# Compression of keys and values: float16 halves under a power-of-two scale in place of 32-bit halves

## The chip, the cores and the metric

The kernel runs on one core of a Trainium2 chip. The metric is the device time of one execution in microseconds; the table below gives the median of three timed runs. A separate profiled execution of the same program gives the trace.

## What is computed

The reference is one inference step of a hybrid decoder layer for 2048 prompt tokens and 8 x 4 sample tokens: a norm, one wide input projection, a sparse attention (compressed, selected and window branches), a gated linear recurrence, gates, an output projection. The part that matters here is the compression of keys and of values into blocks:

```python
def compress(kv, pos, w1, w2):            # CMP_LEN 32, CMP_STRIDE 16, NSA_KV 2, NSA_HD 64, CMP_HID 64
    idx = np.arange(nc)[:, None] * CMP_STRIDE + np.arange(CMP_LEN)[None, :]
    blk = kv[:, idx] + pos[:, None, :]
    blk = jnp.swapaxes(blk, 2, 3).reshape(B, nc, NSA_KV, CMP_LEN * NSA_HD)
    out = jax.nn.silu(blk @ w1) @ w2
```

It runs on keys and on values, for the eight sample sequences (2048 past positions, gathered from pages) and for the prompt: nine sequences for each of the two kinds.

## The kernel before

The whole step is one program. Each product that needs more than half precision is written as three products of halves: high x high, low x high, high x low. The input projection keeps its operands as float16 halves under power-of-two scales (`load_w`, `pow2_scale`). Its matmuls are the program's filling: a generator (`projections`) hands out a few of them at a time, and other parts of the program call `fill(ns)` to put so many nanoseconds of them between their own steps. Lines 480 (token groups) and 399 (feature groups) are these matmuls. ScalarE and VectorE take their results out of two PSUM buffers.

The compression (`compression`, from line 1002) is driven by `along(compression(range(9)), 1900.0)`: after each of its steps 1900 ns of projection are put in. For each kind the weights `w1` are loaded as a 128 x 8 x 128 tile `raw` and cut into the halves `cwh` and `cwl` (lines 1017, 1018). Then, for each of nine sequences:

- the raw rows `xr` (128 x 2048) are gathered (line 996) or loaded (1040), two buffers in turn, and regrouped into `xg` by ScalarE (1045), for every fourth sequence by GpSimd (1043);
- four times, `turn` transposes four 128 x 128 pieces into the PSUM tile `pt` (1052), ScalarE copies it as the high half `Rh` (1056), and VectorE subtracts to get the low half `Rl` (1057); a turn is issued one step before its use;
- six matmuls for each turn (1069), 24 for a sequence, sum into `ph`; these are 432 in all;
- ScalarE and VectorE add the two shifted halves of `ph` into `hb` (1071, 1072), tanh and a small second product follow.

The helper `pow2_scale` transposes a column of row values on TensorE into a PSUM tile (`tp`, one buffer, shared with the projections), takes the maximum, clears the mantissa bits and inverts: one transpose and five small VectorE operations (lines 197 to 205).

The order of each engine's queue is decided by the scheduler of the language when the program is built. It goes by the program's order as priority and by a simulated timeline (`TC_ARGS = {"schedule_with_timeline_sim": True}`), so later work that is ready can move ahead of earlier work that isn't. On the chip the queues then run in that fixed order.

Of the kernel before, what the change touches and what calls it, by code (L numbers as in the profile page):

```python
# [10 lines left out]
F32 = mybir.dt.float32  # L11
F32R = mybir.dt.float32r
F16 = mybir.dt.float16
BF = mybir.dt.bfloat16
I32 = mybir.dt.int32
AF = mybir.ActivationFunctionType
OP = mybir.AluOpType
AX = mybir.AxisListType
# [122 lines left out]
def trunk_kernel(ctx: ExitStack, tc: tile.TileContext, A, O):  # L141
    nc = tc.nc
    pe, ve, ac, gp, sy = nc.tensor, nc.vector, nc.scalar, nc.gpsimd, nc.sync

    def f(ap):
        return ap.bitcast(F32)
# [48 lines left out]
    def pow2_scale(mx, pool, ps, tag):  # L195

        pe.transpose(ps[:, 0:128], mx.to_broadcast([128, 128]), ident)
        un = pool.tile([128, 1], F32, name=tag + "u", bufs=3)
        ve.tensor_reduce(un, ps[:, 0:128], axis=AX.X, op=OP.max)
        ve.tensor_scalar(un, un, TINY, None, op0=OP.max)  # L200
        ui = un.bitcast(I32)
        ve.tensor_scalar(ui, ui, 0x7F800000, None, op0=OP.bitwise_and)
        ve.tensor_scalar(un, un, 2.0 ** -14, None, op0=OP.mult)
        sc = pool.tile([128, 1], F32, name=tag + "s", bufs=3)
        ve.reciprocal(sc, un)
        return sc, un
# [7 lines left out]
    def track(col, src, rows=128):  # L214
        t_ = con.tile([128, 1], F32, name="trk", bufs=4)
        ve.tensor_reduce(t_[:rows], src, axis=AX.X if len(src.shape) == 2 else AX.XY, op=OP.max, apply_absolute_value=True)
        ve.tensor_tensor(mxs[:rows, col:col + 1], mxs[:rows, col:col + 1], t_[:rows], op=OP.max)
# [777 lines left out]
    def gather(dst, cache, b):  # L995
        gp.indirect_dma_start(out=dst, out_offset=None, in_=A[cache][0].rearrange("n (m l) g d -> (n m) (l g d)", l=16),
                              in_offset=bass.IndirectOffsetOnAxis(ap=idx[:, b:b + 1], axis=0))
# [6 lines left out]
    def compression(seqs):  # L1004
        with ExitStack() as st:
            cw = st.enter_context(tc.tile_pool(name="cw", bufs=1, side="right"))
            cp = st.enter_context(tc.tile_pool(name="cp", bufs=1, side="right"))
            cps = st.enter_context(tc.tile_pool(name="cps", bufs=1, space=PSUM, side="right"))
            ctp = st.enter_context(tc.tile_pool(name="ctp", bufs=3, space=PSUM, side="right"))
            for kind in "kv":  # L1010
                raw = cp.tile([128, 2048], F32, name="xr", bufs=2)[:, :1024].rearrange("p (j c) -> p j c", j=8)
                w1 = A["cmp_w1_" + kind][0]
                for a in range(2):
                    sy.dma_start(raw[:, :, a * 64:(a + 1) * 64], w1[a * 1024:(a + 1) * 1024].rearrange("(j p) c -> p j c", p=128))
                wh = cw.tile([128, 8, 128], F32R, name="cwh")
                wl = cw.tile([128, 8, 128], F32R, name="cwl")
                ac.activation(wh, raw, AF.Copy)
                ve.tensor_sub(wl, raw, f(wh))
                w2 = cw.tile([128, 128], F32, name="w2" + kind)
                ve.memset(w2, 0.0)  # L1020
                sy.dma_start(w2[:64, :64], A["cmp_w2_" + kind][0])
                ps = cw.tile([128, 16], F32, name="pos" + kind)
                sy.dma_start(ps, A["cmp_pos_" + kind][0].rearrange("(j a) d -> (a d) j", a=2))
                pc = cps.tile([64, 1], F32, name="p2")
                for l in range(16):
                    mm(pc, raw[:, l % 8, (l // 8) * 64:(l // 8 + 1) * 64], ps[:, l:l + 1], l == 0, l == 15)
                cb = cw.tile([64, 1], F32, name="cb" + kind)
                ve.tensor_copy(cb, pc)
                cn = cw.tile([64, 1], F32, name="cn" + kind)
                ve.tensor_scalar(cn, cb, 0.5, None, op0=OP.mult)  # L1030
                ve.tensor_scalar(w2[:64, :64], w2[:64, :64], 0.5, None, op0=OP.mult)
                hb_ = cw.tile([128, 2, 128], F32, name="hb" + kind)
                ve.memset(hb_, 0.0)
                hb = hb_[:64]
                for s in seqs:
                    xr = cp.tile([128, 2048], F32, name="xr", bufs=2)
                    if s < 8:
                        gather(xr, "cache_cmp_" + kind, s)
                    else:
                        sy.dma_start(xr, O["p_cmp_" + kind][0, 0].rearrange("(m l) g d -> m (l g d)", l=16))  # L1040
                    xg = cp.tile([128, 2, 16, 64], F32, name="xg", bufs=2)
                    if s % 4 == 3:
                        gp.tensor_copy(xg.rearrange("p g l d -> p l g d"), xr.rearrange("p (l g d) -> p l g d", g=2, d=64))
                    else:
                        ac.activation(xg.rearrange("p g l d -> p l g d"), xr.rearrange("p (l g d) -> p l g d", g=2, d=64), AF.Copy)
                    ph = cps.tile([128, 2, 128], F32, name="ph")

                    def turn(j2):
                        pt = ctp.tile([128, 4, 128], F32, name="pt")
                        for a in range(4):  # L1050
                            j, g = j2 * 2 + a // 2, a % 2
                            pe.transpose(pt[:, a], xg[:, g, 2 * j:2 * j + 2].rearrange("p a d -> p (a d)"), ident)  # L1052
                        Rh = cp.tile([128, 2, 2, 128], F32R, name="Rh", bufs=3)
                        Rl = cp.tile([128, 2, 2, 128], F32R, name="Rl", bufs=3)
                        ptv = pt.rearrange("p (j g) m -> p j g m", g=2)
                        ac.activation(Rh, ptv, AF.Copy)
                        ve.tensor_sub(Rl, ptv, f(Rh))
                        return Rh, Rl

                    nxt = turn(0)  # L1060
                    k = 0
                    for j2 in range(4):
                        Rh, Rl = nxt
                        if j2 < 3:
                            nxt = turn(j2 + 1)
                        yield
                        for j in range(2):
                            for l, r in ((wh, Rh), (wl, Rh), (wh, Rl)):
                                mm(ph, l[:, 2 * j2 + j], r[:, j], k == 0, k == 23)  # L1069
                                k += 1  # L1070
                    ac.activation(hb[:, :, :127], ph[64:128, :, 1:128], AF.Copy)
                    ve.tensor_add(hb[:, :, :127], hb[:, :, :127], ph[0:64, :, :127])
                    he = cp.tile([64, 2, 128], F32, name="he")[:, :, :127]
                    ac.activation(he, hb[:, :, :127], AF.Tanh, scale=0.5, bias=cn)
                    ve.tensor_scalar(he, he, 1.0, None, op0=OP.add)
                    ve.scalar_tensor_tensor(hb[:, :, :127], hb[:, :, :127], cb, he, op0=OP.add, op1=OP.mult)
                    yield
                    if kind == "k":
                        p2 = cps.tile([128, 2, 128], F32, name="p2")
                        mm(p2, w2, hb_, True, True)  # L1080
                        p2 = p2[:64]
                        if s < 8:
                            for g in range(2):
                                ve.tensor_copy(kcT[0][g * 64:(g + 1) * 64, s], p2[:, g])
                        else:
                            ve.tensor_copy(kcp, p2)
                            track(1, kcp[:, :, :127], 64)
                    else:
                        p2 = cps.tile([128, 2, 64], F32, name="p2")
                        for g in range(2):  # L1090
                            mm(p2[:, g], hb_[:, g], w2[:, :64], g == 0, True)
                        if s < 8:
                            ve.tensor_copy(vcs[0][:, s].rearrange("p (g d) -> p g d", g=2), p2)
                        else:
                            ve.tensor_copy(vcp, p2)
                            track(2, vcp[:127], 127)
# [1001 lines left out]
    with ExitStack() as s2:  # L2098
        sw, sb = ExitStack(), ExitStack()
        load_x, fill, state = make_projections(s2, sw, sb)  # L2100
# [61 lines left out]
```

## Time and profile before

| what | us |
|---|---|
| median of three timed runs | 2340.65 (2339.75 to 2341.35) |
| the profiled execution | 2322.12 |
| its span in the trace | 2320.2 |
| TensorE busy in the span | 2215.4 (95%) |
| VectorE / ScalarE / GpSimd busy | 1490.3 / 1191.0 / 1005.6 |

Matmuls are pipelined: each record is longer than the time it holds the engine. The pitch, from one start to the next or from a run of equal matmuls divided by their number, tells what one costs. A row of a group of instructions gives the count, the busy time, the mean of one in ns, and the idle time of the engine just before them with what ended it. A row of the chain of waits gives start, length and what the chain went through.

### The profile page before, as it was taken

The numbers are of one execution on the slowest core, as the hardware profiler recorded it, in microseconds if no ns is written. First come the engines' busy times: TensorE is split into PE (matmuls) and PEld (weight loads), VectorE is DVE, ScalarE is ACT, GpSimd is POOL, SyncE is SP. The second block draws the span as 40 slices with busy tenths as digits, with TensorE's granted clock in tenths as the row PEclk, the third lists the DMA queues.
The fourth block names the chain that finished last, engine by engine and source line by source line (L and its number), as shares of the span: only waits on it lengthen the run. The fifth ranks groups of instructions, "written<-read, shape, count | busy, mean of one in ns | idle before, by whom it ended". The sixth has DMA issues, their size and how long they took to land.

```text
span 2320.2 us, 57026 instructions
## 1 busy us (share of the span) xinstructions
PE 2215.4 (95%) x22427; PEld 1537.1 (66%) x22427; DVE 1490.3 (64%) x3780; ACT 1191.0 (51%) x2658; POOL 1005.6 (43%) x1190
## 2 busy tenths in 40 slices
PE   7999999999899989999999898999999999999998
PEld 6898775565686556665665466767667676666765
DVE  8655555756713699777753466767777676766633
ACT  7444333422622277666642366356546565667663
POOL 0100102242700066666610145457557675767763
PEclk9999999999999999999999999999999999999999
DMA  7634323677832443444335634323222121211121
GB/s 235 187 111 121 130 74 128 238 256 253 253 104 79 151 140 125 128 129 136 113 100 139 168 104 107 95 70 94 73 73 78 56 73 50 60 50 48 52 59 45
DMA packets 278388, 271.64 MB, mean 117 GB/s; under 512 B 104576, under 2 KB 248456, under 8 KB 270696
## 3 DMA queue, kind: packets, MB, share of 16 engines
q1 hardware_dynamic: 269608, 230.25, 32.6%
q0 software_dynamic: 8512, 37.75, 4.8%
q8 instruction: 176, 2.88, 0.5%
q14 instruction: 92, 0.75, 0.1%
HBM read 184.40 MB, written 87.74 MB: 117 GB/s over the span
## 4 chain that ended last, share of the span: by engine, by line
PE 71%; DVE 11%; DMA 6%; issue 4%; ACT 3%; SPq 2%; POOL 1%; POOLq 0%; DVEq 0%; ACTq 0%
PE ps L399 16%; PE ps L1926 7%; PE ps L480 7%; PE ps L1894 7%; PE ps L459 5%; PE mx L1647 3%; PE st L1783 3%; PE st L1771 3%; PE ph L1069 2%; PE po L1572 2%; PE po L1575 2%; PE po L1573 2%; PE pt L1052 1%; DMA wraw<-in_w_in_dram 1%; DVE X L770 1%
## 5 line engine op out<-in xcount | busy, mean ns | idle before, releaser
L1566 POOL TENSOR_TENSOR Pl<-P,Ph 128x512 f16<-128x512 f32 x444 | 517.9, 1176 | 335.9 <-ACT Ph L1565 202.9
L1564 ACT ACTIVATE P<-st 128x512 f32<-128x512 f32 x444 | 264.8, 597 | 243.9 <-PE st L1783 186.4
L399 PEld LDWEIGHTS <-wh 128*128 128x128 f16 x2240 | 218.2, 99 | 170.6 <-issue 19.1
L1565 ACT ACTIVATE Ph<-st 128x512 f16<-128x512 f32 x444 | 263.4, 595 | 9.9 <-PE po L1573 6.3
L399 PE MATMUL ps<-xh,wh 128*128 128x512 f16 (+1 forms) x1120 | 231.0, 342 | 7.6 <-DVE row L421 3.9
L399 PE MATMUL ps<-xl,wh 128*128 128x512 f16 (+1 forms) x1120 | 230.5, 340 | 0.0
L399 PE MATMUL ps<-xh,wl 128*128 128x512 f16 (+1 forms) x1120 | 229.8, 340 | 0.0
L1650 DVE TENSOR_REDUCE mps<-mx 128x1 f32<-128x512 f32 (+3 forms) x320 | 185.7, 603 | 51.5 <-PE mx L1647 28.0
L480 PE MATMUL ps<-wh,xh 128*128 128x256 f16 (+1 forms) x680 | 187.7, 276 | 7.6 <-ACT wh L308 4.7
L480 PE MATMUL ps<-wh,xl 128*128 128x256 f16 (+1 forms) x680 | 187.1, 275 | 1.3 <-DVE xl L365 1.3
L480 PE MATMUL ps<-wl,xh 128*128 128x256 f16 (+1 forms) x680 | 187.3, 275 | 0.0
L399 PEld LDWEIGHTS <-wl 128*128 128x128 f16 x1120 | 109.2, 98 | 80.6 <-issue 2.1
L1572 PEld LDWEIGHTS <-Ph 128*128 128x128 f16 x1776 | 141.1, 99 | 31.7 <-DVE otmp L1664 3.8
L731 POOL TENSOR_TENSOR Xo<-Xo,qt 128x256 f32<-128x256 f32 x32 | 31.7, 989 | 280.3 <-ACT Xo L730 280.3
L1573 PEld LDWEIGHTS <-Ph 128*128 128x128 f16 x1776 | 129.6, 97 | 34.3 <-issue 1.1
L480 PEld LDWEIGHTS <-xh 128*128 128x128 f16 x1360 | 130.9, 98 | 23.8 <-issue 2.9
L1650 DVE TENSOR_REDUCE mpw<-mx 128x1 f32<-128x512 f32 (+3 forms) x224 | 102.9, 483 | 43.4 <-PE mx L1649 42.0
L1894 PEld LDWEIGHTS <-xh 128*128 128x128 f16 x1280 | 104.1, 98 | 28.1 <-issue 7.5
L1575 PEld LDWEIGHTS <-Pl 128*128 128x128 f16 x1776 | 94.7, 98 | 21.5 <-POOL Pl L1566 6.3
L1572 PE MATMUL po<-vs,Ph 128*128 128x65 f16 x1088 | 106.6, 193 | 2.4 <-DVE otmp L1664 2.4
L1771 PE MATMUL st<-qb,kbs 128*128 128x512 f16 x272 | 103.6, 381 | 4.0 <-ACT Ph L1565 3.8
L1573 PE MATMUL po<-vs,Ph 128*128 128x64 f16 x1088 | 105.6, 194 | 0.0
(519 smaller groups left out, 5711.8 us busy)
## 6 DMA issues: line engine op xcount, KB each, us to landing
wraw<-in_w_in_dram SPq DMA_DIRECT2D x22, 1024.0 KB
xt<-in_x_prompt_dram SPq DMA_DIRECT2D x32, 512.0 KB
ma_d<-row SPq DMA_DIRECT2D x8, 1040.0 KB
out_y_prompt_dram<-xt SPq DMA_DIRECT2D x16, 512.0 KB
sg<-ma_d SPq DMA_DIRECT2D x56, 128.0 KB
sg<-mb_d SPq DMA_DIRECT2D x56, 128.0 KB
q_d<-row SPq DMA_DIRECT2D x4, 1040.0 KB
lf_d<-row SPq DMA_DIRECT2D x4, 1040.0 KB
```

The source lines that it names most:

```text
L399: mm(ps, l[:, kc], xs(r, t0, n)[:, kc], k == 0, k == 23)
L480: mm(ps, x, w[:, kc], k == 0, k == 23)
L1564: ac.activation(P[:n], ps, AF.Exp, scale=1.0 / QS)
L1565: ac.activation(ph[:n], ps, AF.Exp, scale=1.0 / QS)
L1566: sub.tensor_sub(pl[:n], P[:n], ph[:n])
L1572: mm(po[:, r, :w], ph[:n, rs[r]], v[:n, :w], first and r == 0, False)
L1573: mm(po[:, r, :64], ph[:n, rs[r]], v[:n, w:w + 64], False, False)
L1575: mm(po[:, r, :w], pl[:n, rs[r]], v[:n, :w], False, last)
L1650: ve.tensor_reduce(mp_[:, r, c:c + 1], pmf[:, :n], axis=AX.X, op=OP.max)
L1771: mm(ps, kb, flat(u["b"]), True, False)
L1894: mm(X["ps"], w[:, kc, cs], os_[o][:, kc], k == 0, k == 11)
L1926: mm(X["ps"], X["y"][y][:, kc, i0:i0 + r], W["o", kc // 4][w][:, kc % 4, cs], k == 0, k == 23)
```

## The change

Weights and transposed rows of the compression become float16 high and low halves. The weights get one scale from the largest magnitude of the whole tile. Each sequence gets one from the sums of magnitudes of its rows, which ScalarE forms with a pass over `xr` (its elementwise output, `junk`, isn't used). The copies and subtractions apply the scale, and the scale is undone (`back`) where `ph` is read.

```diff
-                wh = cw.tile([128, 8, 128], F32R, name="cwh")
-                wl = cw.tile([128, 8, 128], F32R, name="cwl")
-                ac.activation(wh, raw, AF.Copy)
-                ve.tensor_sub(wl, raw, f(wh))
+                wh = cw.tile([128, 8, 128], F16, name="cwh")
+                wl = cw.tile([128, 8, 128], F16, name="cwl")
+                mxw = cp.tile([128, 1], F32, name="mxw")
+                ve.tensor_reduce(mxw, raw, axis=AX.XY, op=OP.max, apply_absolute_value=True)
+                scw, unw = pow2_scale(mxw, cw, state["env"]["tp"](), "cx")
+                ac.activation(wh, raw, AF.Copy, scale=scw)
+                ve.scalar_tensor_tensor(wl, raw, scw, wh, op0=OP.mult, op1=OP.subtract)
...
+
+                    junk = cp.tile([128, 2048], BF, name="junk", bufs=1)
+                    mxx = cp.tile([128, 1], F32, name="mxx", bufs=2)
+                    ac.activation(junk, xr, AF.Abs, accum_out=mxx)
+                    sc, un = pow2_scale(mxx, cp, state["env"]["tp"](), "cs")
+                    back = cp.tile([128, 1], F32, name="back", bufs=2)
+                    ve.tensor_scalar(back, un, unw, None, op0=OP.mult)
...
-                        Rh = cp.tile([128, 2, 2, 128], F32R, name="Rh", bufs=3)
-                        Rl = cp.tile([128, 2, 2, 128], F32R, name="Rl", bufs=3)
+                        Rh = cp.tile([128, 2, 2, 128], F16, name="Rh", bufs=3)
+                        Rl = cp.tile([128, 2, 2, 128], F16, name="Rl", bufs=3)
                         ptv = pt.rearrange("p (j g) m -> p j g m", g=2)
-                        ac.activation(Rh, ptv, AF.Copy)
-                        ve.tensor_sub(Rl, ptv, f(Rh))
+                        ac.activation(Rh, ptv, AF.Copy, scale=sc)
+                        ve.scalar_tensor_tensor(Rl, ptv, sc, Rh, op0=OP.mult, op1=OP.subtract)
...
-                    ac.activation(hb[:, :, :127], ph[64:128, :, 1:128], AF.Copy)
-                    ve.tensor_add(hb[:, :, :127], hb[:, :, :127], ph[0:64, :, :127])
+                    ac.activation(hb[:, :, :127], ph[64:128, :, 1:128], AF.Copy, scale=back[64:128])
+                    ve.scalar_tensor_tensor(hb[:, :, :127], ph[0:64, :, :127], back[0:64], hb[:, :, :127], op0=OP.mult, op1=OP.add)
```

## Rows read from the trace of the kernel before

**Rows 1.** The page: engine totals, TensorE in 40 slices, float16 weight loads

```profile
PE 2215.4 (95%) x22427; PEld 1537.1 (66%) x22427; DVE 1490.3 (64%) x3780; ACT 1191.0 (51%) x2658; POOL 1005.6 (43%) x1190
PE   7999999999899989999999898999999999999998
...
L480 PEld LDWEIGHTS <-xh 128*128 128x128 f16 x1360 | 130.9, 98 | 23.8 <-issue 2.9
```

**Rows 2.** Busy time by stretch: length, busy time of each engine, clock, DMA

```profile
core 0: us, PE busy (x) PEld busy (x) DVE busy (x) ACT busy (x) POOL busy (x), PEclk, DMA share, GB/s
85.00:361.00 276.00, 275.96 (x2149) 224.33 (x2149) 149.00 (x391) 109.21 (x180) 22.30 (x19) 1.00 0.38 121
361.00:640.00 279.00, 262.30 (x2266) 158.63 (x2266) 185.63 (x360) 106.28 (x193) 116.47 (x146) 0.98 0.71 237
```

**Rows 3.** The chain of waits within 85 to 361 us, shares by line

```profile
by line: PE ps L480 34.0%; PE ps L399 30.5%; PE ph L1069 18.7%; PE pt L1052 11.5%; PE tp L512 1.5%; PE p L1080 1.4%; PE p L1091 1.2%; PE p L1026 1.0%; PE tp L197 0.2%; issue 0.0%
```

**Rows 4.** Pieces of that chain in order of time: start, length, what

```profile
86.83 2.62 PE ps L480 x24
89.45 0.24 PE ph L1069 x2
...
142.34 0.71 PE ph L1069 x6
...
343.06 0.87 PE pt L1052 x8
```

**Rows 5.** Timeline of TensorE: start, length, instruction, where line 480 follows 1069

```profile
142.77 0.28 PE L1069 MATMUL ph<-Rl,cwh 128*128 128x256 f32 x1
142.90 0.28 PE L480 MATMUL ps<-wh,xh 128*128 128x256 f16 x1
```

**Rows 6.** Groups by line and shape within 85 to 361 us

```profile
L1057 DVE TENSOR_TENSOR Rl<-pt,Rh 128x512 fp32r<-128x512 f32 x72 | 48.5, 687 | 28.3 <-ACT Rh L1056 28.0
L1056 ACT ACTIVATE Rh<-pt 128x512 fp32r<-128x512 f32 x72 | 40.9, 596 | 74.3 <-PE pt L1052 74.2
L1069 PEld LDWEIGHTS ph<-Rh,cwh 128*128 128x128 f32 x144 | 27.4, 190 | 3.2
L1045 ACT ACTIVATE xg<-xr 128x2048 f32<-128x2048 f32 x13 | 24.8, 1905 | 3.5 <-DMA xr<-in_cache_cmp_k_dram,idx 3.5
L1074 ACT ACT_TABLE_LOAD x1 | 1.3, 1283 | 0.0
```

**Rows 7.** The same view: a weight maximum and parts of the scale helper

```profile
L302 DVE TENSOR_REDUCE wmx<-wraw 128x1 f32<-128x2048 f32 x4 | 9.1, 2286 | 7.4 <-DMA wraw<-in_w_in_dram 7.4
L199 DVE TENSOR_REDUCE wxu<-tp 128x1 f32<-128x128 f32 x4 | 1.1, 286 | 0.1
L205 DVE RECIPROCAL wxs<-wxu 128x1 f32<-128x1 f32 x4 | 0.6, 162 | 0.1
```

**Rows 8.** The same view over the whole run: scaled copies, scaled products, summing passes

```profile
L421 DVE SCALAR_TENSOR_TENSOR row<-ps,ug,row 128x512 f32<-128x512 f32 x12 | 9.0, 751 | 0.4
L350 ACT ACTIVATE junk<-xt 128x1024 bf16<-128x1024 f32 x16 | 16.9, 1055 | 8.8 <-DMA xt<-in_x_prompt_dram 6.9 <-DVE rsx L354 1.2 <-ACT junk L350 0.3
L414 ACT ACTIVATE row<-ps,us 128x512 f32<-128x512 f32 x12 | 8.2, 687 | 28.6 <-PE ps L399 28.5
L350 ACT ACTIVATION_READ_ACCUMULATOR junk<-xt 128x1 f32 x16 | 3.1, 191 | 0.0
```

**Rows 9.** Timeline of ScalarE at the start of compression, and its last regrouping copy

```profile
79.07 1.05 ACT L1017 ACTIVATE cwh<-xr 128x1024 fp32r<-128x1024 f32 x1
82.10 1.91 ACT L1045 ACTIVATE xg<-xr 128x2048 f32<-128x2048 f32 x1 [0.31 <-DMA xr<-in_cache_cmp_k_dram,idx]
86.43 1.08 ACT L1056 ACTIVATE Rh<-pt 128x512 fp32r<-128x512 f32 x2 [2.03 <-PE pt L1052]
...
321.33 1.90 ACT L1045 ACTIVATE xg<-xr 128x2048 f32<-128x2048 f32 x1
```

**Rows 10.** Waits of TensorE over the run: total us, times, longest

```profile
PE p L802 <- POOL X L774: 8.9, 5, 6.6
```

## The prediction

> **What bounds the kernel now.** I read the busy table first. TensorE is busy for 2215 of 2320 us, 95%, and only six of the forty slices lie under nine tenths [rows 1]. A busy TensorE says little by itself, so the second view is the stretch in which the changed code runs. Compression covers 85 to 361 us, and there TensorE is busy for 275.96 of 276.00 us at full clock, while VectorE has 149 us of work, ScalarE 109 and GpSimd 22 [rows 2]. The third view settles it: the chain of waits cut to this stretch lies wholly on TensorE. Projection matmuls hold 34.0 and 30.5% of it, the compression's own matmuls (line 1069) 18.7%, its transposes (line 1052) 11.5%; issue has 0.0% and no other engine appears [rows 3]. So the stage ends when its TensorE instructions have gone by, one after another. Only what alters the count or the pitch of TensorE instructions, or what makes TensorE wait where it waits for nothing now, can move the end. ScalarE and VectorE have time to spare: the copies that make `Rh` sat idle 74 us waiting for transposes, and those that make `Rl` 28 us waiting for `Rh` [rows 6].
>
> A microsecond gained here should reach the end, since the steps after compression follow it in program order and TensorE is nearly full there as well: 262 of 279 us in the next stretch [rows 2].
>
> **Matmuls, 432 of them.** 18.7% of 276 us is 51.6 us, so one takes 119.5 ns; six in a row take 0.71 us, 118 ns each [rows 3, 4]. Float16 matmuls of the same 256 columns stand beside them: 24 projection matmuls in 2.62 us, 109.2 ns each [rows 4]. With float16 operands the 432 should take that pitch: 432 x 10.3 ns = 4.4 us less (3.9 by the row of six). The first float16 matmul behind a group of six begins 0.13 us after the last of them, against a pitch of 0.109 [rows 5]; if that goes too, at 72 groups, it is up to 72 x 0.02 = 1.4 us. I take half, 0.7, as one row is thin.
>
> A weight load in front of each matmul is 190 ns long today, and 98 ns where the operands are float16 [rows 1, 6]. The difference times 432 is 40 us, but it isn't a term: 190 ns of loading already fits under a pitch of 119 ns, so loads run in the shadow of earlier matmuls. [...]
>
> **New TensorE work.** Each of the 18 sequences (nine for keys, nine for values) gets one 128x128 transpose for its scale, and each of the two weight sets one. Eight such transposes take 0.87 us [rows 4], 109 ns each: 20 x 0.109 = 2.2 us more. They wait for the sum of magnitudes, and behind them in TensorE's queue stands everything else, the projections included, so this is the wait to watch.
>
> **New ScalarE work.** The pass that sums magnitudes is 128x2048. The same kind with 1024 elements takes 1055 ns and its read of the sum 191; the regrouping copy of 2048 elements takes 1905 [rows 6, 8]. So about 1.9 + 0.2 = 2.1 us, 18 times: 38 us. A per-row scale on the 72 `Rh` copies lifts them from 596 to some 687 ns, as a scaled copy of that shape shows [rows 6, 8]: 72 x 0.09 = 6.5 us. ScalarE goes from 109 to about 154 of 276 us. That is cover enough on average; TensorE sees it only if a copy is late.
>
> Whether the magnitude function swaps ScalarE's table no row shows. The stretch has one load under the tanh, 1.3 us long [rows 6]; the bound is 0 to two loads per sum, 36 x 1.28 = 46 us of ScalarE, 200 of 276 us in all. I take 0, as the 85 copies of lines 1045 and 1056 go to and fro with the tanh of line 1074 on that one load. [...]
>
> **New VectorE work.** One scale is a reduction of 128 columns (286 ns) and four small operations near 160 ns, and `back` one more [rows 7]: 0.29 + 5 x 0.16 = 1.1 us, 20 us for 18. The 72 `Rl` become a scaled subtraction, 687 to at most 751 ns [rows 6, 8]: 4.6 us. With the weights' reductions VectorE goes from 149 to some 177 of 276 us. All of it lies beside TensorE. Queued behind the scale on VectorE are `Rl` and the evacuations of projections.
>
> **How early the scale is ready.** In the steady state it is far ahead. The last regrouping copy runs at 321.3 us and its sequence's first transposes at 343.1 [rows 4, 9], 21.7 us later. The sum needs only the same raw rows as that copy, so 2.1 + 0.1 + 1.1 us fit several times. The gather of the sequence after next now waits for a second reader of `xr`, 2 us later; as its data lies 20 us waiting, it costs nothing. If that cover were gone, 18 x 3.3 us = 59 us would be the price.
>
> The exception is the first sequence. Weights: raw at 79.1, a reduction of 1024 elements (half of 2286 ns [rows 7]) to 80.3, scale to 81.5, `cwh` to 82.6. Then the regrouping copy to 84.5, the sum to 86.6, scale to 87.8, so the first `Rh` starts there instead of at 86.43 [rows 9], and `Rl` is done near 89.3. Before, 24 projection matmuls ended and the first matmul on `Rh` started at 89.45 [rows 4]. So it just fits: 0 to 1.4 us, I take 0.3.
>
> **Sum.** -4.4 - 0.7 + 2.2 + 0.3 = -2.6 us. The profiled execution took 2322.12 us, so 2319.5. The median of the timed runs, 2340.65, is 0.8% above it; TensorE's work scales along, and -2.6 us on it gives 2338.0. A measurement of this kernel can tell about 0.2%, 4.7 us, from no change, so this is a gain that would count as none.
>
> **Rivals.**
> 1. *ScalarE's long passes make TensorE wait (slower).* Between the transposes of one step and the matmuls that use them stand one filling of 1.9 us and six matmuls, 2.6 us. Needed are 0.44 for four transposes, 0.69 for `Rh`, 0.75 for `Rl`: 1.9. Slack 0.7. A 2.1 us sum that starts just before `Rh` overdraws it by 1.4 us. All 18 would cost 25 us; it decides from about five hits, where -2.6 + 7 is past +4.4. At ten hits: 2340.65 - 2.6 + 14 = 2352. Against it: fourteen regrouping copies of 1.9 us do the same today and TensorE waited for none of them, because later projections move forward in the order. For it: copy and sum come due together, 4 us in a block. Chance 0.18, most of it slower.
> 2. *The order of the rest shifts.* The queues of all engines are ordered from a simulated timeline of the whole program. 2.6 us less here moves each later step against the transfers and against GpSimd. TensorE loses 105 us in all, in single waits such as 8.9 us for GpSimd in the recurrence [rows 10] and 17 us in the sample attention's stretch [rows 2]. Up to a tenth of it, 5 to 10 us, can fall either way: with the saving 2328 to 2335, chance 0.20; against it 2343 to 2349, chance 0.10.
> 3. *The pitch doesn't fall.* If 119 ns belonged to the output or the 256 columns and not to the 32-bit operands, only the transposes remain: +2.5 us, 2343.1. The float16 rows beside them speak against it [rows 4]. Chance 0.04.
>
> **How the numbers follow.** The forecast has 0.48: mostly within 0.2%, while with the full 1.4 us of the joints and some luck it passes -4.7 (0.12 of the 0.48). Faster: 0.12 + 0.20 = 0.32. Same: 0.36 from the forecast, 0.04 from rival 1 with few hits, 0.03 from rival 3: 0.43. Slower: 0.14 + 0.10 + 0.01 = 0.25. The range runs from 2329, rival 2 in our favour, to 2352, rival 1 at ten hits; some 0.2 lies beyond. The forecast's own range is 2335 to 2342.
>
> **What would show it.** In the profile after, the line of matmuls on `Rh` should come at six in 0.65 us, weight loads near 98 ns; the stretch from the first to the last of them should be about 2.6 us shorter, TensorE still without a wait in it, ScalarE's busy time up by some 45 us and VectorE's by 28. The sums should start 15 us or more ahead of their transposes. Wrong would be: waits of TensorE on `Rh`, `Rl`, the scale transpose or a projection's evacuation (rival 1); an equal compression stretch with a changed time behind it (rival 2); table loads between sums; a first matmul on `Rh` later than 91 us.

## The result and the profile after

The changed kernel takes 2350.93 us (median of five, 2349.16 to 2355.61) beside 2340.65 us before: a ratio of 1.0051, interval 1.0033 to 1.0069. It is 10 us slower. The time lies inside the predicted range, but the sign of the forecast (-2.6 us) is wrong.

The profiled execution of after took 2349.16 us and that of before 2322.12, which is 27 us apart and not 10: the profiled run of before lies 18 us under its median. Sums over stretches of these two traces therefore overstate the loss, and the sizes below go by single executions; where the loss sits is checked further down in other runs.

The same view as [rows 6], over 76 to 365 us of after: groups by line and shape, busy us and mean ns, then idle time before them and what ended it.

```profile
L1067 DVE SCALAR_TENSOR_TENSOR Rl<-pt,css,Rh 128x512 f16<-128x512 f32 x72 | 51.7, 744 | 21.1 <-ACT Rh L1066 20.8
L1066 ACT ACTIVATE Rh<-pt,css 128x512 f16<-128x512 f32 x72 | 46.0, 684 | 41.8 <-PE pt L1062 25.9 <-DVE css L205 6.8 <-DVE back L1055 5.8
L1052 ACT ACTIVATE junk<-xr 128x2048 bf16<-128x2048 f32 x18 | 34.3, 1906 | 12.3 <-PE tp L197 9.0 <-PE ps L480 2.5 <-DMA xr<-in_cache_cmp_v_dram,idx 0.8
L1079 PEld LDWEIGHTS <-cwh 128*128 128x128 f16 x288 | 28.5, 99 | 7.0 <-issue 1.3
L1055 DVE TENSOR_SCALAR back<-csu,cxu 128x1 f32<-128x1 f32 x18 | 3.5, 195 | 0.0
L1052 ACT ACTIVATION_READ_ACCUMULATOR junk<-xr 128x1 f32 x18 | 3.4, 187 | 0.0
L1084 ACT ACT_TABLE_LOAD x1 | 1.3, 1283 | 0.0
```

Every piece was priced well: `Rh` at 684 ns, `Rl` at 744, the sum at 1906 + 187, weight loads at 98 to 99, and no sum brought a table load: over the stretches of the two kernels there are the same two, 1283 ns each, under the tanh (line 1084) and at line 374. In the chain of waits, six compression matmuls now take 0.66 us, where [rows 4] has 0.71:

```profile
159.51 0.66 PE ph L1079 x6
```

The view of [rows 2] of after, first the old stretch, then three that are cut at the same pieces of work in both kernels: the compression, what follows up to the first gate projection (line 459), and the rest.

```profile
core 0: us, PE busy (x) PEld busy (x) DVE busy (x) ACT busy (x) POOL busy (x), PEclk, DMA share, GB/s
85.00:361.00 276.00, 272.61 (x2167) 215.16 (x2167) 172.74 (x512) 152.05 (x219) 25.56 (x19) 1.00 0.39 121
...
85.00:364.00 279.00, 275.61 (x2190) 217.51 (x2190) 173.28 (x513) 152.05 (x219) 25.56 (x19) 1.00 0.38 120
364.00:1192.00 828.00, 778.45 (x7475) 500.11 (x7475) 544.23 (x1146) 398.33 (x1149) 341.04 (x536) 0.97 0.48 157
1192.00:2347.00 1155.00, 1109.11 (x12234) 760.57 (x12231) 729.20 (x2075) 629.86 (x1238) 634.86 (x627) 0.98 0.29 80
```

The same two later stretches in the kernel before (its first is the 276 us of [rows 2]):

```profile
361.00:1170.00 809.00, 767.16 (x7482) 494.78 (x7482) 544.19 (x1147) 399.21 (x1150) 346.60 (x537) 0.99 0.49 161
1170.00:2320.00 1150.00, 1106.81 (x12237) 759.70 (x12235) 731.21 (x2075) 630.69 (x1237) 634.12 (x627) 0.99 0.29 80
```

Three things are to be seen. ScalarE's 152 and VectorE's 173 us are what was forecast (154 and 177). The compression got no shorter: 279 for 276 us. And the greater part of the loss lies behind it, 828 for 809 and 1155 for 1150 us, in code that the diff doesn't touch and with nearly the same number of matmuls (7475 and 7482). Of the 19 us in the middle stretch, 11 are TensorE's busy time, at a mean granted clock of 0.97 where it was 0.99 (in the traces it stood at 0.50 for 44 us of this stretch, and for 17 us before), and 8 are idle time.

One new wait there is plain. TensorE's waits in 364 to 650 us of after (total us, times, longest):

```profile
PE p L802 <- POOL X L774: 8.5, 2, 6.4
PE pkt L1293 <- DVE kts L1296: 5.3, 1, 5.3
```

The transposes of the sample attention's keys wait once for 5.3 us, at 404 us, for VectorE's copy of an earlier one. The longest wait of that line in the same stretch of before was 1.0 us.

### The profile page after: what moved, and what is told of

Its sections match the earlier page's. It is cut to its first block, busy times and chain, and to the rows that moved or that the text cites. A ratio compares the mean times of both kernels' runs of the same rounds, so it can differ in the third digit from the quotient of the medians.

```text
span 2347.4 us, 57206 instructions
## 1 busy us (share of the span) xinstructions
PE 2228.1 (95%) x22447; PEld 1535.9 (65%) x22447; DVE 1512.4 (64%) x3900; ACT 1230.5 (52%) x2693; POOL 1003.4 (43%) x1190
## 4 chain that ended last, share of the span: by engine, by line
PE 69%; DVE 13%; DMA 6%; issue 4%; ACT 4%; POOL 1%; SPq 1%; another core or an unknown queue 0%; POOLq 0%; ACTq 0%; DVEq 0%
PE ps L399 15%; PE ps L1936 8%; PE ps L1904 7%; PE ps L480 6%; PE ps L459 6%; PE st L1793 3%; PE st L1781 3%; PE mx L1657 3%; DMA wraw<-in_w_in_dram 2%; PE po L1585 2%; PE po L1582 2%; PE po L1583 2%; PE ph L1079 2%; DVE X L770 1%; PE pt L1062 1%
## 5 line engine op out<-in xcount | busy, mean ns | idle before, releaser
L399 PE MATMUL ps<-xh,wh 128*128 128x512 f16 (+1 forms) x1120 | 235.8, 347 | 4.3 <-DVE row L421 2.6
```

Of the source, the lines that this page charges most:

```text
L399: mm(ps, l[:, kc], xs(r, t0, n)[:, kc], k == 0, k == 23)
```

## Experiments

Each difference is between two kernels timed on the same chip. From chip to chip the kernel before took 2327 to 2341 us, so differences are given, with the ratio's interval. All of them but those of the text's order are under 1%.

**The kernel before again, and a null edit.** The second adds one 128x1 clearing per sequence on VectorE and nothing else.

> The kernel before, unchanged, timed against itself. All theories expect a ratio of 1.000 within 0.001. Its profile is what is open: the execution that was profiled took 2322 us where the timed runs took 2340, so this one should show what a usual execution of 2340 us looks like, and where its 18 us more lie: in the sample attention (380 to 580 us), in the recurrence (580 to 1220 us), or spread evenly. If they lie in single stalls, stalls of that kind are no part of the change.

Measured: 2328.29 beside 2327.53 us, ratio 1.0008 (0.9999 to 1.0017). On this chip the kernel takes 2328 us as a rule, and the profiled execution took 2327; so where the 18 us lie that the profile of before lacks stays open.

```diff
+                    nul = cp.tile([128, 1], F32, name="nul", bufs=2)
+                    ve.memset(nul, 0.0)
```

> The kernel before with one memset of a 128x1 tile on VectorE more in each of the 18 sequences of the compression, 60 to 150 ns each, read by nothing: about 2 us of VectorE's spare time and nothing on TensorE. 'The added work costs': no change, ratio 1.000 within 0.001. 'The later order costs': the order of the later queues shifts with it, and the whole moves by 3 us or more in either direction.

Measured: 2328.03, ratio 1.0005 (0.9997 to 1.0014). No change. Its queues stand in exactly the order of before but for the 18 clearings, so it is no test of the order, and it shows that not every edit makes a new one. The clearings, 59 ns each, all ran ahead of the stage (76.2 to 77.9 us), so it doesn't test small VectorE work within the stage either.

**The halves alone, and the added work alone.** The first takes the change with constant scales: no sum of magnitudes, no joining transposes, no chain.

```diff
-                    ac.activation(junk, xr, AF.Abs, accum_out=mxx)
-                    sc, un = pow2_scale(mxx, cp, state["env"]["tp"](), "cs")
...
+                sc = cw.tile([128, 1], F32, name="sc")
+                ve.memset(sc, 2.0 ** 8)
+                back = cw.tile([128, 1], F32, name="back")
+                ve.memset(back, 2.0 ** -20)
```

> The changed kernel with constant scales in place of the measured ones: no sum of magnitudes, no scale transposes, no chain on VectorE; float16 halves as in the change. Both theories expect the 432 matmuls at 0.109 us each and the compression stage 4 to 5 us shorter. 'The added work costs': the whole is then 4 to 5 us faster than before (ratio 0.998), and 13 to 15 us faster than the changed kernel. 'The later order costs': the stage is shorter by 4 to 5 us, but the whole lands anywhere from 6 us faster to 12 us slower, since the order of the later queues is made anew here too.

Measured: 2335.96 beside 2327.53 us, +8.4; ratio 1.0035 (1.0021 to 1.0050). Slower, although TensorE has the same matmuls at a shorter pitch. The stage was expected 4 to 5 us shorter by either theory and came out 2 us longer (stretches below). TensorE's busy time in it is 2 us less with 11 more matmuls, but TensorE's transposes wait once, for 4.0 us, for VectorE's low half `Rl`, in a kernel without a scale to wait for:

```profile
PE pt L1059 <- DVE Rl L1064: 4.0, 1, 4.0
```

The second keeps the 32-bit halves and adds the weights' maximum, the sums, the transposes and the chain, whose scales nothing uses.

> The kernel before with its 32-bit halves, and with all the added work (weight maximum, sums of magnitudes, 20 scale transposes, the chains on VectorE), whose scales are computed and not applied. 'The added work costs': 20 transposes are 2.2 us and waits of TensorE in the compression 4 us or more, the stage is 6 us longer and the whole 10 us or more slower (ratio 1.004 to 1.007). 'The later order costs': the stage is 2 to 6 us longer, and the whole differs from that by several us either way.

Measured: 2345.90 beside 2327.53 us, +18.4; ratio 1.0082 (1.0069 to 1.0095): more than the whole change. So the parts don't add up, and neither is "the cost". Their stretches, cut at the same pieces of work: the kernel before on that chip,

```profile
85.00:362.00 277.00, 276.14 (x2148) 224.18 (x2148) 149.12 (x391) 109.20 (x180) 22.58 (x19) 1.00 0.38 120
362.00:1171.00 809.00, 769.16 (x7486) 497.16 (x7485) 543.85 (x1150) 399.02 (x1151) 348.41 (x537) 0.99 0.48 161
1171.00:2325.00 1154.00, 1108.46 (x12234) 760.65 (x12232) 732.02 (x2074) 630.36 (x1237) 634.58 (x626) 0.98 0.28 80
```

the halves alone,

```profile
85.00:364.00 279.00, 273.90 (x2159) 215.27 (x2159) 156.62 (x393) 118.48 (x182) 23.45 (x19) 0.99 0.37 119
364.00:1179.00 815.00, 772.78 (x7477) 497.12 (x7475) 543.48 (x1146) 396.45 (x1135) 345.64 (x533) 0.98 0.48 159
1179.00:2336.00 1157.00, 1109.89 (x12240) 760.81 (x12237) 731.08 (x2076) 631.37 (x1253) 636.79 (x631) 0.98 0.28 80
```

and the work alone.

```profile
85.00:367.00 282.00, 278.74 (x2169) 226.58 (x2168) 168.23 (x508) 143.16 (x218) 21.71 (x19) 1.00 0.37 118
367.00:1186.00 819.00, 773.13 (x7565) 498.12 (x7564) 545.21 (x1158) 399.25 (x1152) 343.59 (x537) 0.98 0.48 159
1186.00:2343.00 1157.00, 1106.74 (x12153) 758.17 (x12150) 729.89 (x2064) 629.91 (x1235) 635.18 (x626) 0.99 0.28 80
```

All the stage's own differences (+2 and +5) are smaller than what comes behind it (+6 and +3; +10 and +3). Two theories were left: the order of the queues behind the stage, which a simulated timeline of the whole program decides, or something of the change itself that reaches beyond it (the smaller tiles' places in memory, the added work's effects).

**The order held.** With the timeline switched off, the queues follow the program's text and its priorities. In four kernels built so, GpSimd's queue and at least the last 33,597 of some 38,000 instructions on TensorE's stand in the same order: on these two engines only the compression differs. Each of the four was timed four times, and the differences between them carry a standard error of 1.5 to 2 us.

```diff
-TC_ARGS = {"schedule_with_timeline_sim": True}
+TC_ARGS = {"schedule_with_timeline_sim": False}
```

> The kernel before with its queues ordered by the order of the program text and its priorities, not from the simulated timeline; nothing is left out. It is the base of three others built the same way, in which the queues behind the compression stage (all of GpSimd's; of TensorE's the last 33597 of 37975 instructions) come in the same order. By itself it may well be 1 to 3 per cent slower than the kernel before (2350 to 2400 us), since no timeline has placed anything; what counts is the difference of the other three from it.

Measured: 2453.11 us, ratio to the kernel before 1.0541 (1.0523 to 1.0559). The order alone is worth 126 us; more than was expected.

> The 16-bit halves under constant scales, without sum of magnitudes, without the two joining transposes and without the chain (the scale by rows is left out), queues ordered like the base. Theory order: it gains what the pitch gives, -2 to -6 us against the base (the same kernel with queues from the timeline lost 8 us). Rival work: it loses again, +5 to +10 us.

Measured: 2446.20 us, 6.9 under that base: theory order, and a little more than the pitch was thought to give. Its compression stretch, beside that of the base below (300 us, 289.91 busy), has 3.8 us less of busy time (the sum has 4.4 for the pitch) and 3.2 us less of idle time:

```profile
85.00:378.00 293.00, 286.07 (x2180) 216.22 (x2178) 155.26 (x400) 119.13 (x182) 22.24 (x18) 0.99 0.35 111
```

> The 32-bit halves with all the added work, whose scales are not used, queues ordered like the base. Theory order: +2 to +6 us (20 transposes of 109 ns are 2.2 us on TensorE, and a wait or two); with queues from the timeline it lost 18 us. Rival work: +14 us or more again.

Measured: 2450.48 us, 2.6 under it (not clear of no difference), less than theory order had put it, and 21 us from what it did in the timeline's order.

> The whole change with queues ordered like the base just named, so that behind the compression stage nothing stands in another order. Theory order (the timeline placed later work otherwise, and that costs the 12 us): the difference to the base falls to what the stage itself gives, -3 to +4 us. Rival work (the added sums, chains and transposes, or the smaller halves themselves, cost it wherever they stand): +9 to +15 us, as in the change.

Measured: 2458.56 us, 5.5 above the base: outside both ranges, though by 1.5 us from the nearer one, which is less than the error. Its stretches tell where. The base,

```profile
85.00:385.00 300.00, 289.91 (x2175) 228.55 (x2175) 150.46 (x397) 110.05 (x182) 22.51 (x18) 0.99 0.34 108
385.00:1237.00 852.00, 785.76 (x7582) 506.22 (x7580) 544.10 (x1181) 411.73 (x1181) 350.17 (x538) 0.97 0.47 153
1237.00:2452.00 1215.00, 1128.23 (x12128) 759.23 (x12126) 715.45 (x2036) 627.32 (x1208) 634.72 (x625) 0.98 0.27 75
```

and the whole change in the same order:

```profile
85.00:395.00 310.00, 293.48 (x2200) 220.03 (x2198) 176.29 (x518) 151.26 (x217) 22.50 (x18) 0.98 0.33 105
395.00:1249.00 854.00, 786.08 (x7581) 507.63 (x7580) 543.46 (x1180) 412.20 (x1181) 349.87 (x538) 0.97 0.47 153
1249.00:2459.00 1210.00, 1125.12 (x12128) 757.55 (x12125) 712.07 (x2036) 627.53 (x1208) 634.69 (x625) 0.98 0.27 75
```

Behind the compression nothing is lost: 854 for 852 us, 1210 for 1215, TensorE's busy time equal to 0.3 us in the middle. With the order held, no loss is seen beyond the stage; the 19 us of the middle stretch above are gone. (TensorE idles 66 us there in this order, against 42 in the timeline's, so a small delay of another engine could hide.) What it does lose is 10 us inside the stage, where the two partial kernels gained 7 and 1. Of the 10, 6.4 are idle time (16.5 for 10.1) and 3.6 busy time, with 25 more matmuls. TensorE's waits there:

```profile
PE ph L1079 <- ACT Rh L1066: 10.3, 9, 3.8
PE p L1101 <- DVE csu L202: 2.0, 1, 2.0
PE tp L512 <- ACT to L488: 1.3, 6, 0.3
```

The largest of the base's 10.1 us is another one:

```profile
PE ph L1069 <- DVE Rl L1057: 5.9, 2, 4.9
```

ScalarE's waits in 70 to 400 us of the whole change tell what `Rh` waited for:

```profile
ACT junk L1052 <- PE tp L197: 15.6, 10, 3.8
ACT Rh L1066 <- DVE back L1055: 13.0, 5, 5.8
...
ACT Rh L1066 <- DVE css L205: 6.2, 2, 4.1
```

The waits for `css`, the scale, and for `back` (19.2 us together) can stand in neither partial kernel: one has no scale to wait for, the other doesn't use it. They come from joining the two. The sum's own wait, with `Rh` behind it, stands in the work alone as well, 8.3 us there, and TensorE waited only 1.0 us for `Rh` in it. How much of the 10.3 us comes by which of the two, these traces don't separate.

**The order alone.** The same kernel, with 10 or 50 ns more or less projection work behind each step of the compression; the work stays the same (ScalarE alone has one table load more at 1890 and two at 1950), but the timeline then orders much of what stands behind otherwise; the last third of TensorE's matmuls keeps its order. The edit for 1910:

```diff
-            along(compression(range(9)), 1900.0)
+            along(compression(range(9)), 1910.0)
```

> The kernel before, with the same instructions, and 10 ns less of projection work (1890 for 1900) placed behind each step of the compression: its queues come out in another order from the stage on, nothing else differs. Theory order (what stands behind the stage depends on small shifts of the simulated timeline, and the order before is a good one): it differs from the kernel before by several us, +3 to +15. Rival (the order is worth little, the change's loss is its own work): within 2.5 us of the kernel before.

> The kernel before, 10 ns more of projection work (1910 for 1900) behind each step of the compression: the same instructions in another order from the stage on. Theory order: it differs from the kernel before by several us, +3 to +15, and not by the same as the run with 1890. Rival: within 2.5 us.

> The kernel before, 1850 for 1900 ns of projection work behind each step of the compression: another order, the same instructions. Theory order: 0 to +15 us against the kernel before, like the draws at 1890 (+3.5) and 1910 (+12). Rival (1910 was an outlier): within 4 us.

> The kernel before with 1950 for 1900: another order. Theory order: 0 to +15 us; rival: within 4 us.

And the same edits on the changed kernel:

> The whole change with 1890 for 1900 behind each step of the compression. Theory order: another draw of the order, 2325 to 2350 us, that is, several us from the change's own 12 us on either side. Rival: the change's own +10 to +14 us against the kernel before, within 2.5 us.

> The whole change with 1910 for 1900 behind each step of the compression. Theory order: another draw of the order, 2325 to 2350 us. Rival: the change's own +10 to +14 us against the kernel before, within 2.5 us.

> The whole change with 1850 for 1900: another order. If the change costs nothing of its own, its draws spread like those of the kernel before, 0 to +15 us with a mean near +5; if it has a cost of its own of 5 us or more, they stay at +6 to +20.

> The whole change with 1950 for 1900: another order. As for 1850: 0 to +15 us if the change costs nothing of its own, +6 to +20 if it has a cost of its own of 5 us or more.

Measured, in us against the kernel before on the same chip, the ratio's interval in brackets (at 1900: the kernel before itself, and the change from its own measurement):

| ns per step | before | changed |
|---|---|---|
| 1850 | +4.6 (1.0010 to 1.0035) | +13.5 (1.0042 to 1.0077) |
| 1890 | +3.5 (0.9997 to 1.0022) | +9.6 (1.0024 to 1.0060) |
| 1900 | 0 | +10.3 (1.0033 to 1.0069) |
| 1910 | +12.1 (1.0042 to 1.0078) | +5.7 (1.0010 to 1.0033) |
| 1950 | +20.1 (1.0068 to 1.0115) | +7.1 (1.0019 to 1.0043) |

The kernel before speaks clearly at 1910 and 1950, +12 and +20 us, the last beyond the range given for it; 1850 lies only 0.6 us past what the rival allowed, and the interval of 1890 reaches to no change. The draws of the changed kernel separate less. 1890, with +9.6, lies where the rival put it, 1910, with +5.7, under the rival's range, and 1850 and 1950 fit both ranges that were given for them.

Ten nanoseconds more, without any other change, cost the kernel before 12 us, about as much as the change did. And the middle stretch grew in the same way. Stretches of the kernel before with 1910, an execution on a chip where the kernel before took 2340.5 us, so that its sizes beside the trace of before (28 us apart, not 12) are again too large:

```profile
85.00:361.00 276.00, 275.52 (x2143) 223.99 (x2143) 149.31 (x391) 109.93 (x182) 22.87 (x19) 1.00 0.37 121
361.00:1186.00 825.00, 771.32 (x7486) 497.63 (x7484) 538.43 (x1132) 395.75 (x1133) 342.89 (x529) 0.98 0.47 157
1186.00:2349.00 1163.00, 1113.60 (x12243) 763.11 (x12240) 733.81 (x2090) 632.79 (x1255) 637.79 (x635) 0.98 0.28 79
```

The compression takes its 276 us as ever, the middle stretch 825 instead of 809, the rest 1163 instead of 1150. Among TensorE's waits stands the one from 404 us of after, at 403 us, in a kernel with no scale and no half precision in its compression:

```profile
PE pkt L1283 <- DVE kts L1286: 5.5, 1, 5.5
```

This wait is a mark of an order, not the loss itself: the two slowest kernels in the timeline's order, the work alone and the kernel before with 1950, have nothing of it beyond 0.3 us, and the halves alone with 1910 (below), the fastest, have 3.8 us. The order reaches into the stage, too: in the kernel before with 1890 TensorE waits there once for 4.0 us.

```profile
PE ph L1069 <- DVE hbv L1072: 4.0, 1, 4.0
```

And it can undo the loss of the middle stretch with the whole change in place; with 1950 that takes 803 us, less than the 809 of before (the loss of 7 us lies elsewhere):

```profile
367.00:1170.00 803.00, 761.51 (x7447) 492.87 (x7446) 537.37 (x1143) 398.75 (x1137) 350.97 (x533) 0.99 0.49 160
```

The mean of the five draws is +8.1 us for the kernel before and +9.2 for the changed one. The scatter is 8 and 3 us, so the difference of 1 us carries a standard error of about 4 (8 and 3 over the root of five, added in squares). The two kernels can't be told apart once the order is averaged out; a gain of the forecast's size, or a loss of several us, isn't excluded.

**The halves alone in two more orders.** At 1900 they had lost 8.4 us.

> The 16-bit halves under constant scales (no scale by rows, no sum, no joining transposes, no chain), with 1890 for 1900: another order. If the saved pitch reaches the end, draws of this kernel lie 4 to 7 us under those of the kernel before (mean +8), so near +2 us, anywhere from -7 to +13; if the smaller halves themselves cost something behind the stage, it stays at +8 or more.

> The same with 1910 for 1900: another order. As for 1890: -7 to +13 us, around +2, if the saved pitch reaches the end; +8 or more if the smaller halves cost something behind the stage.

Measured: +3.9 us (ratio 1.0008 to 1.0030) and -3.8 us (0.9974 to 0.9997). The loss doesn't stay: the three draws have a mean of +2.8, where the kernel before has +5.2 at the same three steps. Each three scatter by 6 us, so that whether the saved pitch reaches the end isn't decided by them. The one at 1910 is the only kernel that came out under the kernel before, by 0.14%, with constant scales that don't fit every input; no order of the whole change beat it.

## Why the prediction was wrong

Two steps failed. The scale was taken to be ready far ahead, with a joint of 0.3 us as its whole cost to TensorE; the stage had 3.2 us of new waits, and the saving of 2.2 us (4.4 less the transposes) was gone. And the stage's difference was taken to reach the end; the order of what stands behind, made anew, moved the kernel before alone by up to 20 us. That the time fell into the range is luck: the upper end was worked out from ten hits of a long sum, which is not what happened.

**What bounds the stage: right.** TensorE, busy for 275.6 of 279.0 us, and only its pitch, its count and its waits.

**The prices: right.** The pitch fell to that of the float16 neighbours (0.66 us for six), the groups above cost what was estimated, and the weight loads of 98 ns instead of 190 brought no 40 us, as said. Abs loaded no table: with the 18 sums the stretch has the two loads that it had before, the one of [rows 6] and one of line 374 (1283 ns, at 239 us of after and 236 of before), which the prediction didn't count.

**"In the steady state it is far ahead": wrong.** The step looked at when the raw rows arrive, and not at what the chain has to pass. A scale goes through the queues of three engines, ScalarE's twice, and each link stands in its queue behind other work. The last sequence of after, in lines of ScalarE's sum, TensorE's transpose, the end of VectorE's chain (first and last start):

```profile
L1052 ACT ACTIVATE junk<-xr x18: 1892/1910/1912, 85.2 to 314.6; 128x2048 bf16<-128x2048 f32 x18
```

```profile
L197 PE MATMUL tp<-ident,mxx x18: 272/272/273, 88.5 to 344.5; 128*128 128x128 f32 x18
```

```profile
L205 DVE RECIPROCAL css<-csu x18: 149/164/165, 90.7 to 346.0; 128x1 f32<-128x1 f32 x18
```

ScalarE's timeline at that point:

```profile
346.27 1.93 ACT L1066 ACTIVATE Rh<-pt,css 128x512 f16<-128x512 f32 x3 [0.21 <-DVE css L205]
```

The sum started 30 us ahead of its transpose, as forecast (15 or more). But the transpose came 1.8 us before `Rh` began, and `Rh` waited 0.2 us. Over the stage `Rh` waited 6.8 us for the scale and 5.8 for `back`, which stands behind it on VectorE (groups above). The sum itself has a wait that the working doesn't name: `mxx` has two buffers, and the sum after next waits until the transpose has read the first, 9.0 us in all, with `Rh` behind it on ScalarE. In the timeline's order TensorE felt little of that:

```profile
PE tp L512 <- DVE csu L199: 1.3, 1, 1.3
PE tp L512 <- ACT to L488: 1.0, 1, 1.0
PE ph L1079 <- DVE Rl L1067: 0.9, 1, 0.9
```

That is 3.2 us of waits in a stage that had none in the trace of before, and they consume the saving of 4.4 - 2.2. Only the first is for the scale's chain by name; a wait for `Rl` of 0.7 us stands in the kernel before run again, too. The stage's 279 instead of 276 us also hold 10 projection matmuls more (some 1.7 us; 485 of line 399 instead of 475) and 12 small ones of line 1029 (some 0.7 us), which stood ahead of 85 us before. With these and 19 of the transposes (2.1 us) counted, TensorE's 275.6 us of busy time instead of 276.0 make the pitch worth 4.8 us, by estimate, beside the 4.4 + 0.7 of the sum. In the order of the text the wait for `Rh` was 10.3 us: this is the first rival, in the size that it gave for five to ten hits, but through a late scale and the two buffers of `mxx`, not through the length of the sums.

**The first sequence: wrong in order, free of charge.** The working put the weights' copy ahead of the first sum. ScalarE's timeline of after, beside [rows 9]:

```profile
83.39 1.91 ACT L1048 ACTIVATE xg<-xr 128x2048 f32<-128x2048 f32 x1 [1.01 <-DMA xr<-in_cache_cmp_k_dram,idx]
85.21 1.89 ACT L1052 ACTIVATE junk<-xr 128x2048 bf16<-128x2048 f32 x1
...
87.45 1.13 ACT L1020 ACTIVATE cwh<-xr,cxs 128x1024 f16<-128x1024 f32 x1
...
90.91 1.84 ACT L1066 ACTIVATE Rh<-pt,css 128x512 f16<-128x512 f32 x3
```

The first `Rh` starts at 90.9 instead of 86.4, and the first matmul on it at 93.4, past the 91 that was named as a sign. TensorE took projections in the meantime; none of the waits above lies there.

**"A microsecond gained here should reach the end": this step decided.** While the order holds it is right to a few us: the halves alone took 7 us from the stage (293 for 300) and 6.9 from the whole by the medians (11 in the two traces), and the whole change added 10 to the stage and 5.5 to the whole (7 in the traces). It doesn't hold where a timeline decides the order anew. A shift of 10 ns per step moved the whole by 12 us, so 2.6 us in the stage are no forecast for the end. The second rival said just this, but with 5 to 10 us and 0.30 in all, and with the better chance on the side of a gain. It should have carried most of the probability: the order draws of before spread over 0 to +20 us, up to eight times the 2.6 us that the sum was about. Nothing in the rows of the trace tells its direction. All nine other draws of the two kernels lay above the order of the kernel before (one of them, 1890, within its error), so the order that it has is one of the better ones, and a new draw loses more often than it gains; that could not be read from its profile.

**What stays open.** Why the timeline places the copy of `kts` late in some orders wasn't followed into its decisions. The own cost of the change is known only as 1 us with a standard error of 4 over five orders, and as 5.5 with one of 2 in the order of the text, where the late scale cost more. A join with more buffers for `mxx`, or further ahead in TensorE's queue, wasn't tried.

## What to carry to other kernels

Where queues are ordered from a simulated timeline, an edit of a few us in an early stage can be a new draw for what stands behind it (here 10 ns per step moved the whole by 12 us). Measure first what the order is worth (change one filling constant by half a per cent, hold the order fixed), and judge the edit by the mean over several draws or with the order held. And a small value that one engine sums, another joins and a third finishes is as late as its last queue lets it be (here the sum began 30 us ahead of its transpose, and the copy still waited 0.2 us for the scale): look for its place in each queue, for the buffers that tie its first step to its last, and for who stands behind the reader.

## What was not expected of the hardware

A program that is 95% TensorE-busy moved by 0.2 to 0.9% in three of four other orders of the same work (0.1% in the fourth, within its error), and by 5.4% in the order of the text. Part of it is the clock: in the middle stretch of after, TensorE's mean granted clock was 0.97 where before had 0.99. In the trace of after it stood at 0.50 in ten pieces of 3.4 or 6.8 us there, 44 us in all, and in four of before, 17 us; at 0.50 eight matmuls of line 399 (128x272) took 1.92 us, at 1.00 1.09 us (at 614.4 and 616.1 us of after). The stretch of after had 49.6 us without a matmul instead of 41.8 (the stretch less TensorE's busy time), and nearly the same number of matmuls (7475 and 7482) took 11 us more of busy time. The loss of the stretch, 19 us, is thus more than twice its added waiting (8 us); what lowered the clock, and whether the waits had a share in it, these runs don't show.
